# Issuing the eight late stores of each group of results from ACT's queue and no longer from SP's

## The chip, the cores and the metric

The kernel runs on one core of one Trainium2 chip. The metric is the device time of one execution in microseconds (us). The version before takes 1500.18 us (the median of three runs, 1498.26 to 1500.47).

Engines are called as in the profile: PE multiplies matrices, DVE does elementwise work on vectors, ACT applies a function or a scale while it copies, POOL does a few elementwise additions, and SP does no arithmetic; until now it is the queue from which nearly all transfers are issued. A transfer (DMA) is started by an instruction in some engine's queue. The instruction waits there, in order with the rest of that queue, until what it needs is ready; then it hands the transfer to the DMA engines and the queue goes on. The transfer lands some time later.

## The reference

```python
x: (8, 2048, 2048) float32      w: (2048, 2048) float32
cs   = cumsum(x, axis=1)
diff = cs - (cs shifted by one row)
out  = matmul(diff, w)          # (8, 2048, 2048) float32
```

The difference of a running sum is the input itself, so what has to be computed is x times w: 16384 rows of x, each of 2048 numbers, times a matrix of 2048 by 2048.

## The kernel before

The 16384 rows are 128 tiles of 128 rows. The first tiles go through code of their own (a plain product while w is loaded, then two transitional groups). From tile 12 on the work is done in 29 **groups** of four tiles, called g, h, k and l. One group is a product of two-by-two blocks that is computed by seven block products (`P1` to `P7`, the Strassen-Winograd scheme) in place of eight. Most of them are split again by the same scheme into seven quarter products (`P7.p1` to `P7.p7` and so on), so that PE has less to multiply and DVE, ACT and POOL have more to add.

For each tile of a group the following steps run:

- `load` fetches a tile of x in two halves into slots of the buffer `F` (line 113, SP).
- `weigh0` and `weigh1` run over the two halves on ACT and give sums of absolute values (line 125). From them comes a scale for each row (`scale`, `recip`, `unit`, on POOL and DVE).
- `narrow0` and `narrow1` scale the tile and round it to 16 bits, in place in `F` (line 172, ACT).
- `turn0` and `turn1` are transfers that transpose the rounded tile from `F` into one of the tiles `x00` to `x31` (line 185, SP). A slot of `F` can be loaded again when the transposes that read it have landed.

The results of a group are 16 pieces of 128 by 512 numbers: `C11`, `C12`, `C21` and `C22`, each with `g0`, `g1`, `h0` and `h1`. A piece is collected in one of seven buffers `c0` to `c6`. ACT copies the first partial product into the buffer (`keep`), DVE adds others (`add`), and at last the piece is stored (`put`, line 614). The list of free buffers is a queue: `put` hands its buffer back, and the next step that needs one takes the oldest, so that the next writer of a buffer has to wait until the store that reads it has landed. The same seven buffers also serve as scratch for the copies that ACT makes of partial products (`P7.c1`, `P7.c5`, `P7.c6`, `P7.c7`, line 1086).

Eight of the 16 pieces are scaled **late** (the list `LATE`): they are collected without their row scale, by plain copies (`keep`, line 1116) and plain additions (`add`, line 1127), and ACT multiplies the finished piece by the row scale in place (`last`, line 600). The other eight are scaled at each step, and the last to touch them is DVE.

The order of all this is written out by hand in the table `ORDER`. It names each step of a group and how many groups ahead of the others it runs; the program goes through the table once per group. The helper `after` chains the instructions of each engine in that order, so every engine's queue is in the order of the table. The last group has no late pieces and an order of its own (`END_ORDER`).

Of the kernel before, what the change touches and what calls it, by code (L numbers as in the profile page):

```python
# [10 lines left out]
def kernel(  # L11
# [6 lines left out]
    nc = tc.nc  # L18
    P = 128
# [7 lines left out]
    NB = 512  # L27
# [19 lines left out]
    out2 = out.rearrange("b s d -> (b s) d")  # L47
# [38 lines left out]
    def after(engine, ask):  # L86
        if engine in last:
            with tc.issue_after(last[engine].ins):
                said = ask()
        else:  # L90
            said = ask()
        last[engine] = said[-1] if isinstance(said, tuple) else said
        return said
# [100 lines left out]
    with ExitStack() as head:  # L194
# [103 lines left out]
        def put(c, rows, columns, queue=nc.gpsimd):  # L298
            return queue.dma_start(out2[rows, columns], c)
# [86 lines left out]
        with tc.issue_after(whole_max.ins):  # L386
            for c, rows, columns in done:
                put(c, rows, columns)
# [21 lines left out]
        def left_over(ps):  # L410
            for ko in range(KO):
                after(
                    "pe",
                    lambda: nc.tensor.matmul(
                        ps,
                        xP[:, PLAIN - 1, ko, :],
                        (B11, B21)[ko // KH][ko % KH][:, 1, :],
                        start=(ko == 0),
                        stop=(ko == KO - 1),
                    ),  # L420
                )
            c = turned_x[3][0].rearrange("p k m -> p (k m)").bitcast(f32)
            after("act", lambda: nc.scalar.activation(c, ps, COPY, scale=uw))
            rows = ds((PLAIN - 1) * P, P)
            after("sp", lambda: put(c, rows, ds(NB, NB), nc.sync))
# [37 lines left out]
        for c, rows, columns in (done[0], done[3]):  # L463
            after("sp", lambda: put(c, rows, columns, nc.sync))
# [134 lines left out]
    def keep(c, p, u):  # L599
        after("act", lambda: nc.scalar.activation(c, p, COPY, scale=u))  # L600
# [9 lines left out]
        for n in range(2):  # L610
            add(c[n], p[n], u)

    def put(c, t, at):
        after("sp", lambda: nc.sync.dma_start(out2[ds(t * P, P), ds(at * NB, NB)], c))  # L614
        free.append(c)

    store = put
# [370 lines left out]
    class Group:  # L988
# [145 lines left out]
        def put(self, c):  # L1134
            n = 2 * (c[2] == "2") + int(c[4])
            if c in self.late:
                self.step(f"last.{c}", lambda: keep(self.at[c], self.at[c], unit[self.row(c)]))
            self.step(f"put.{c}", lambda: put(self.at.pop(c), self.row(c), n))

        def plan(self):  # L1140
            tiles = self.tiles
# [226 lines left out]
```

## Time and profile before

| what | value |
|---|---|
| median of three runs | 1500.18 us (1498.26 to 1500.47) |
| the profiled execution | 1502.03 us, of which the span from the first to the last instruction is 1500.3 us |
| granted PE clock, mean over the span | 0.997 |
| busy share of the span | PE 96%, DVE 94%, ACT 77%, POOL 35% |
| DMA issues on SP | 246 loads of x, 246 transposes, 492 stores out of `c` buffers, and those of the first tiles |
| DMA | 351.65 MB, mean 234 GB/s; the queue fed by SP was in work for 85.0% of the time of 16 DMA engines |

The groups are alike: between 245 us and 1450 us there are 27 passes through the table, 44.6 us each. So what one pass shows can be multiplied by 27, if the groups of rows show the same wait that many times.

In the rows, a line number is that of the kernel before; "idle before" or a bracket behind an instruction is the time its engine stood still before it, with what ended that wait. "SPq" is SP's queue of DMA issues; "ACTq" is the sequencer of ACT, which handles waits and issues ahead of the arithmetic. `W` is the space of the weights, `flow`, `inner` and `S` are scratch.

### The profile page before, as it was taken

To read this page: it belongs to the slowest core of one execution; us is meant where nothing else is said; L and a number is where in the kernel's file an instruction comes from. 1 tells how busy PE (TensorE), PEld (TensorE's weight loads), DVE (VectorE), ACT (ScalarE), POOL (GpSimd) and SP (SyncE) were. 2 spreads that over 40 slices of the span, in tenths; PEclk is the share of its full clock that TensorE was granted. 3 is DMA by queue.
4 is the path that set the end of the run, shared out by engine and by line. 5 is a ranking of instruction groups with operands and counts; after the bars stand their busy time and mean duration, and the time that the engine had idled before them with its cause. 6 is when DMAs were issued, how large, how long until landed. Compare 5 with 4: busy or idle time off the path is not lost.

```text
span 1500.3 us, 21260 instructions
## 1 busy us (share of the span) xinstructions
PE 1442.9 (96%) x6563; PEld 634.9 (42%) x6563; DVE 1405.8 (94%) x2280; ACT 1154.3 (77%) x1786; POOL 520.0 (35%) x509
## 2 busy tenths in 40 slices
PE   8999989999999999999999999999999999999997
PEld 3444434444444444444444444444444444444443
DVE  7998899999999999999999999999999999999998
ACT  5887467778778788778788778788778777788883
POOL 0111234334434334434334334334334334343342
PEclk9999999999999999999999999999999999999999
DMA  9999758988988988888988888888888988889883
GB/s 363 359 240 282 200 156 223 239 230 219 249 229 219 254 230 224 242 234 222 245 219 227 242 230 229 249 212 241 237 227 238 248 207 232 231 226 247 232 217 126
DMA packets 377761, 351.65 MB, mean 234 GB/s; under 512 B 274800, under 2 KB 274800, under 8 KB 377520
## 3 DMA queue, kind: packets, MB, share of 16 engines
q1 hardware_dynamic: 377088, 348.47, 85.0%
q0 software_dynamic: 560, 1.84, 0.3%
q8 instruction: 51, 0.84, 0.2%
q14 instruction: 62, 0.51, 0.1%
HBM read 150.99 MB, written 134.22 MB: 190 GB/s over the span
## 4 chain that ended last, share of the span: by engine, by line
PE 41%; DVE 28%; DMA 16%; issue 6%; ACT 6%; SPq 2%; POOL 0%; ACTq 0%; DVEq 0%
PE b L592 28%; PE b L573 10%; DVE flow L958 8%; DMA F<-in_x_dram 7%; DVE b L1061 6%; DMA out_dram<-c 6%; DVE c L1127 6%; DVE c L603 4%; PE b L289 3%; DMA x<-F 2%; ACT c L600 2%; DVE x L563 2%; DVE inner L563 1%; SPq L614 1%; ACT waste L125 1%
## 5 line engine op out<-in xcount | busy, mean ns | idle before, releaser
L592 PE MATMUL b<-W,x 128*128 128x512 f16 x2124 | 508.3, 379 | 28.1 <-DVE c L1127 17.0
L592 PEld LDWEIGHTS <-x 128*128 128x128 f16 x2952 | 286.8, 98 | 389.6 <-issue 43.0
L1127 DVE TENSOR_TENSOR c<-b,c 128x512 f32<-128x512 f32 x504 | 325.1, 679 | 2.1 <-ACT c L1116 1.6
L125 ACT ACTIVATE waste<-F 128x1024 uint8<-128x1024 f32 x246 | 259.6, 1055 | 78.7 <-DMA F<-in_x_dram 77.2
L592 PEld LDWEIGHTS <-inner 128*128 128x128 f16 x1996 | 191.7, 98 | 268.0 <-DVE inner L563 25.2
L592 PE MATMUL b<-W,inner 128*128 128x512 f16 x1176 | 289.0, 380 | 9.1 <-DVE b L1061 4.8
L172 ACT ACTIVATE F<-F,of 128x1024 f16<-128x1024 f32 x246 | 282.8, 1150 | 15.9 <-DVE of L156 12.8
L573 PE MATMUL b<-W,x 128*128 128x512 f16 x1216 | 278.0, 379 | 4.1 <-DVE x L563 4.1
L603 DVE SCALAR_TENSOR_TENSOR c<-b,of,c 128x512 f32<-128x512 f32 x286 | 207.8, 742 | 30.4 <-ACT c L600 24.2
L600 ACT ACTIVATE c<-b,of 128x512 f32<-128x512 f32 x268 | 180.2, 679 | 72.1 <-issue 26.6
L561 POOL TENSOR_TENSOR x<-x,x 128x512 f16<-128x512 f16 x87 | 128.9, 1482 | 274.1 <-DVE inner L563 258.4
L1116 ACT COPY c<-b 128x512 f32<-128x512 f32 x224 | 127.6, 582 | 116.2 <-DVE c L603 41.2
L563 DVE TENSOR_TENSOR x<-x,x 128x1024 f16<-128x1024 f16 (+1 forms) x330 | 200.3, 613 | 16.5 <-DMA x<-F 13.4
L592 PE MATMUL b<-flow,x 128*128 128x512 f16 x820 | 210.3, 379 | 0.2
L958 DVE TENSOR_TENSOR flow<-W 128x2048 f16<-128x2048 f16 x145 | 201.9, 1392 | 0.1
L1061 DVE TENSOR_TENSOR b<-b,c 128x512 f32<-128x512 f32 x290 | 192.3, 691 | 4.8 <-ACT c L1086 3.4
L561 POOL TENSOR_TENSOR inner<-inner,x 128x512 f16<-128x512 f16 x58 | 89.0, 1535 | 292.6 <-DVE inner L563 287.2
L573 PEld LDWEIGHTS <-x 128*128 128x128 f16 x1216 | 118.3, 98 | 149.5 <-DVE x L563 9.4
L561 POOL TENSOR_TENSOR inner<-x,inner 128x512 f16<-128x512 f16 x87 | 125.6, 1443 | 121.2 <-DVE inner L563 69.8
L600 ACT ACTIVATE c<-c,of 128x512 f32<-128x512 f32 x224 | 155.9, 718 | 1.1 <-DVE c L1127 1.1
L142 POOL TENSOR_SCALAR of<-of 128x1 f32<-128x1 f32 x112 | 96.4, 861 | 123.6 <-ACT waste L125 123.6
L592 PE MATMUL b<-inner 128*128 128x512 f16 x472 | 116.4, 379 | 0.0
(78 smaller groups left out, 959.2 us busy)
## 6 DMA issues: line engine op xcount, KB each, us to landing
F<-in_x_dram SPq DMA_DIRECT2D x246, 512.0 KB, 5.8
out_dram<-c SPq DMA_DIRECT2D x492, 256.0 KB, 3.2
W<-in_w_dram SPq DMA_DIRECT2D x32, 512.0 KB, 9.7
W<-in_x_dram SPq DMA_DIRECT2D x16, 256.0 KB, 7.2
x<-F SPq DMA_TRANSPOSE x246, 3.3
out_dram<-o POOLq DMA_DIRECT2D x5, 256.0 KB, 4.1
out_dram<-o SPq DMA_DIRECT2D x5, 256.0 KB, 3.5
xP<-in_x_dram SPq DMA_DIRECT2D x1, 1024.0 KB, 5.7
```

The source lines that it names most:

```text
L125: lambda: nc.scalar.activation(waste, where[t][i], ABS, scale=1.0 / ROW, accum_out=sums_of[t][:, i : i + 1],),
L172: lambda: nc.scalar.activation(narrowed(t)[:, ds(i * NH, NH)], where[t][i], COPY, scale=s),
L561: after("pool", lambda: nc.gpsimd.tensor_tensor(dst.all, p.all, q.all, op))
L563: after("dve", lambda: nc.vector.tensor_tensor(dst.all, p.all, q.all, op))
L573: said = nc.tensor.matmul(to[n], a[k], b[k][:, n, :], start=(first and k == 0), stop=(k == KH - 1), skip_group_check=True,)
L592: said = nc.tensor.matmul(to, a[k], b[k], start=(first and k == 0), stop=(k == 3), skip_group_check=True)
L600: after("act", lambda: nc.scalar.activation(c, p, COPY, scale=u))
L603: after("dve", lambda: nc.vector.scalar_tensor_tensor(c, p, u, c, MUL, ADD))
L958: after("dve", lambda: nc.vector.tensor_tensor(in_twos(flow), x, y, op))
L1061: after("dve", lambda: nc.vector.tensor_tensor(t, p, s, ADD))
L1116: after("act", lambda: nc.scalar.copy(to, p))
L1127: after("dve", lambda: nc.vector.tensor_tensor(to, p, to, ADD))
```

## The change

`put` gets an argument for the queue. The eight late pieces are stored from ACT's queue, chained behind the ACT instruction that precedes their `put` in the table; the other eight stay on SP. Nothing else is edited: the table, the buffers, the sizes and the arithmetic are as before. There are 28 groups with late pieces, so 224 of the 492 stores move. The last group, which has none, is as it was.

```diff
-    def put(c, t, at):
-        after("sp", lambda: nc.sync.dma_start(out2[ds(t * P, P), ds(at * NB, NB)], c))
+    def put(c, t, at, by="sp"):
+        queue = dict(sp=nc.sync, act=nc.scalar)[by]
+        after(by, lambda: queue.dma_start(out2[ds(t * P, P), ds(at * NB, NB)], c))
         free.append(c)
...
             if c in self.late:
                 self.step(f"last.{c}", lambda: keep(self.at[c], self.at[c], unit[self.row(c)]))
-            self.step(f"put.{c}", lambda: put(self.at.pop(c), self.row(c), n))
+            by = "act" if c in self.late else "sp"
+            self.step(f"put.{c}", lambda: put(self.at.pop(c), self.row(c), n, by))
```

Two places of the instruction order matter for what follows; both are in the pass whose rows are shown later (778 us to 823 us of the trace). The first is SP's queue where the second half of a group's results leaves and the tiles g and h of a later group are loaded. Here `F<-in_x_dram` is a load (two per tile), `out_0_dram<-c3_759` the store of buffer `c3`, and `x31_70<-F_62` a transpose. Before:

```order
L185 DMA_TRANSPOSE x30_69<-F_62 128x8x128
L185 DMA_TRANSPOSE x31_70<-F_62 128x8x128
L614 DMA out_0_dram<-c3_759 128x512
L614 DMA out_0_dram<-c0_747 128x512
L113 DMA F_62<-in_x_dram 128x1024 x2
L614 DMA out_0_dram<-c4_763 128x512
L614 DMA out_0_dram<-c5_767 128x512
L614 DMA out_0_dram<-c6_771 128x512
L113 DMA F_62<-in_x_dram 128x1024 x2
L614 DMA out_0_dram<-c1_751 128x512
L185 DMA_TRANSPOSE x00_63<-F_62 128x8x128
```

And now:

```order
L185 DMA_TRANSPOSE x30_69<-F_62 128x8x128
L185 DMA_TRANSPOSE x31_70<-F_62 128x8x128
L113 DMA F_62<-in_x_dram 128x1024 x4
L615 DMA out_0_dram<-c1_751 128x512
L185 DMA_TRANSPOSE x00_63<-F_62 128x8x128
```

The five stores of `c3`, `c0`, `c4`, `c5` and `c6` (the pieces C11h1, C21h1, C12g1, C21g1 and C11g1) have left SP's queue, and the four half loads of tiles g and h stand directly behind the transposes.

The second place is ACT's queue over the same stretch. `c0_747<-b0_784` is a copy of PSUM bank 0 into `c0`; `waste` is the output of `weigh` that nobody reads; the line numbers of the new kernel are one higher than before from line 615 on. Before:

```order
L600 ACTIVATE c6_771<-c6_771,of_6129 128x512
L600 ACTIVATE c5_767<-c5_767,of_5978 128x512
L125 ACTIVATE waste_61,of_6502<-F_62 128x1024
L1116 COPY c0_747<-b0_784 128x512
L125 ACTIVATE waste_61,of_6502<-F_62 128x1024
L1086 COPY c4_763<-b1_785 128x512
L1116 COPY c5_767<-b5_789 128x512
L1086 COPY c6_771<-b4_788 128x512
L1086 COPY c4_763<-b1_785 128x512
L172 ACTIVATE F_62<-F_62,of_6502 128x1024
L125 ACTIVATE waste_61,of_6574<-F_62 128x1024
L600 ACTIVATE c6_771<-b7_791,of_6351 128x512
```

And now:

```order
L600 ACTIVATE c6_771<-c6_771,of_6129 128x512
L600 ACTIVATE c5_767<-c5_767,of_5978 128x512
L125 ACTIVATE waste_61,of_6502<-F_62 128x1024
L615 DMA out_0_dram<-c5_767 128x512
L1117 COPY c0_747<-b0_784 128x512
L125 ACTIVATE waste_61,of_6502<-F_62 128x1024
L1087 COPY c4_763<-b1_785 128x512
L615 DMA out_0_dram<-c6_771 128x512
L1117 COPY c5_767<-b5_789 128x512
L1087 COPY c6_771<-b4_788 128x512
L1087 COPY c4_763<-b1_785 128x512
L172 ACTIVATE F_62<-F_62,of_6502 128x1024
```

The store of `c6` now stands two instructions ahead of the copy that overwrites `c6` (`P7.c5`), in the same queue, and behind the copy `P7.c1` into `c4`; the store of `c5` stands behind `weigh0` of tile g.

## The prediction

> **What bounds the kernel now.** I read the stretches first (does one engine fill the time?), then the waits of the repeating part, then the instructions of one pass through the table, engine by engine, and last the chain of work. The table by stretches, for the 27 equal passes from 245 to 1450 us; the columns behind the length are busy us of PE, PE's weight loads, DVE, ACT and POOL:
>
> ```profile
> core 0: us, PE busy (x) PEld busy (x) DVE busy (x) ACT busy (x) POOL busy (x), PEclk, DMA share, GB/s
> 245.00:1450.00 1205.00, 1168.43 (x5310) 513.12 (x5309) 1143.58 (x1886) 960.58 (x1515) 463.55 (x454) 1.00 0.87 232
> ```
>
> PE is busy for 1168.4 of 1205 us. Its idle time there is 36.6 us, 1.35 us a pass, so nothing that this change does to the repeating part can gain more than 36.6 us. The question is which of PE's short stops hang on a store or a load. The waits of the same stretch (us in total, times, longest), and below them one of SP's own queue:
>
> ```profile
> ACT waste L125 <- DMA F<-in_x_dram: 72.5, 62, 3.1
> ...
> ACT c L1116 <- DMA out_dram<-c: 23.8, 20, 3.3
> DVE c L603 <- ACT c L600: 22.9, 25, 2.4
> ...
> ACT c L1086 <- DMA out_dram<-c: 10.4, 31, 0.6
> ```
>
> ```profile
> SPq L614 <- ACT c L600: 79.6, 78, 4.0
> ```
>
> ACT waits for loads, and for stores that must land before their buffer is overwritten; DVE waits for an ACT copy once in nearly every pass (25 times). SP stands 79.6 us in front of stores whose scaling on ACT isn't done. One pass shows how these hang together. SP's queue:
>
> ```profile
> 778.14 2.62 SPq L185 DMA_TRANSPOSE x<-F  x2
> 781.39 0.81 SPq L614 DMA_DIRECT2D out_dram<-c  x2
> 782.30 0.90 SPq L113 DMA_DIRECT2D F<-in_x_dram  x2
> 783.24 3.70 SPq L614 DMA_DIRECT2D out_dram<-c  x3
> 786.98 1.51 SPq L113 DMA_DIRECT2D F<-in_x_dram  x2
> ```
>
> The five stores at 781.39 and 783.24 are C11h1, C21h1, C12g1, C21g1 and C11g1, all late. After C12g1 the queue stands until 786.1, when ACT has scaled C21g1, and only then come C11g1 and the loads of tile h. ACT over the same time:
>
> ```profile
> 784.76 1.33 ACT L600 ACTIVATE c<-c,of 128x512 f32<-128x512 f32 x2
> 787.70 1.06 ACT L125 ACTIVATE waste<-F 128x1024 uint8<-128x1024 f32 x1 [1.61 <-DMA F<-in_x_dram]
> ...
> 789.23 1.06 ACT L125 ACTIVATE waste<-F 128x1024 uint8<-128x1024 f32 x1
> ...
> 790.73 0.59 ACT L1086 COPY c<-b 128x512 f32<-128x512 f32 x1 [0.36 <-DMA out_dram<-c]
> 791.22 0.59 ACT L1116 COPY c<-b 128x512 f32<-128x512 f32 x1
> 791.91 1.10 ACT L1086 COPY c<-b 128x512 f32<-128x512 f32 x2
> ...
> 795.70 1.06 ACT L125 ACTIVATE waste<-F 128x1024 uint8<-128x1024 f32 x1 [1.64 <-DMA F<-in_x_dram]
> ...
> 796.75 0.67 ACT L600 ACTIVATE c<-b,of 128x512 f32<-128x512 f32 x1
> ```
>
> Two waits for loads, 1.61 us for tile g and 1.64 us for tile h, and a copy (790.73, `P7.c1`) that waits for C12g1 to land. The copy at 796.75 (`keep.C22g1`) is the one that DVE and through it PE wait for:
>
> ```profile
> 797.46 0.75 DVE L603 SCALAR_TENSOR_TENSOR c<-b,of,c 128x512 f32<-128x512 f32 x1 [1.10 <-ACT c L600]
> ```
>
> ```profile
> 788.57 1.89 PE L592 MATMUL b<-W,x 128*128 128x512 f16 x8
> ...
> 797.95 1.02 PE L592 MATMUL b<-W,x 128*128 128x512 f16 x4 [0.38 <-ACT c L1086]
> ...
> 808.57 5.34 PE L592 MATMUL b<-W,x 128*128 128x512 f16 x24 [0.57 <-DVE c L1127]
> ```
>
> So in each pass one late load of tile h makes ACT late, ACT makes DVE late by 1.10 us, and PE loses 0.38 and 0.57 us behind them. That is where the change is worth something or nothing.
>
> **What the change removes.** SP loses five stores in this place and with them the stand until 786.1. The loads of tile g can go when the transposes are issued, at 780.8 (778.14 + 2.62), 1.5 us before 782.30. Those of tile h need the slots of `F` that the same two transposes read:
>
> ```profile
> x<-F SPq DMA_TRANSPOSE x246, 3.3
> ```
>
> A transpose lands 3.3 us after its issue; the second is issued at about 779.5, so tile h's loads go at about 782.8, 4.2 us before 786.98. Even if the time from the first issue to the last landing stays 8.7 us (786.98 to 795.70), the second half lands at about 791.5, before ACT asks for it at 794.1 (795.70 less 1.64). Both waits for loads go, in this sum.
>
> **What is late next: ACT's own store.** C11g1 is now issued from ACT behind `P7.c1`, and two instructions later `P7.c5` overwrites its buffer. I call X the start of `P7.c1`, L the time from issue to landing, D the start of `P7.c5`: D = X + L + 0.1 (the semaphore, about what the trace leaves between landing and start). Before, X is 790.73 and D is 791.91; the end of `keep.C22g1` (796.75 + 0.67 = 797.42) is 5.51 us after D, of which 1.64 us is the wait for the load. Without that wait it is D + 3.87. DVE is ready at 796.36 (797.46 less 1.10). So DVE's wait is gone for D up to 792.5, and is what it was at D = 793.55: **the change gains while X + L is below 793.45, and loses above.**
>
> X: `P7.c1` needs PE's first four of the eight products at 788.57 (789.6 with the semaphore), C12g1's landing, and `weigh1` of tile g in front of it on ACT. With tile g's loads 1.5 us earlier `weigh0` is bound by the end of the two scalings (784.76 + 1.33 = 786.1), and `weigh1` ends by 789.2. So X lies between 789.6 and the 790.73 of now. I take 789.6, PE's bound, since the loads move by more than the 1.1 us between them.
>
> L is not shown for a store from ACT. The rows nearest to it, all stores of the repeating part and then C21g1 and C11g1 alone (issue ns, then us to landing, each as min, median, max):
>
> ```profile
> L614 SPq DMA_DIRECT2D out_dram<-c x424: 332/408/1805, 250.9 to 1448.0; - x142
> DMA to landing us min/median/max: 2.3/3.3/8.8
> ```
>
> ```profile
> L614 SPq DMA_DIRECT2D out_dram<-c x2: 343/388/432, 786.1 to 786.5; - x2
> DMA to landing us min/median/max: 5.0/5.2/5.3
> ```
>
> The bounds are 2.3 and 5.3. I take the median, 3.3: by 789.6 the loads that these two stood behind have had their 1.5 to 4.2 us of lead. Then D = 789.6 + 3.3 + 0.1 = 793.0, `keep.C22g1` ends at 796.87, and DVE waits 0.5 us in place of 1.1. **0.55 us a pass, in the 25 passes that have the wait: 14 us.** PE can follow: its two stops are 0.95 us together. At L = 2.3 the whole 22.9 us of the row goes.
>
> The page "DMA: Bandwidth & Descriptors" of the Trainium skill (section "Queues, rings and completion order") says that SP and ACT each have a ring of their own on the same 16 DMA engines, and that an engine goes round the rings packet by packet. By that rule a store from ACT is not behind SP's loads, and the sum holds or comes out better; in the trace all these transfers were in one ring, so it doesn't show it.
>
> **The issue on ACT.** 224 stores at a median of 0.41 us are 91 us that move from SP to ACT. I cost them at nothing, because each stands behind at least one ACT instruction that isn't the scaling it waits for, and ACT's sequencer runs ahead of its arithmetic. In the chain of work ACTq handles the waits of two later instructions while the `weigh1` of 795.70 still runs and `keep.C22g1` hasn't begun:
>
> ```profile
> 796.07 0.02 ACTq L1086
> ...
> 796.38 0.02 ACTq L125
> ```
>
> The shortest cover is a copy of 0.59 us over 0.41 us. Without the cover, two issues (C21g1 and C11g1) lie on the way to D: 0.82 us a pass. Three of the eight stores also inherit a wait for a semaphore that a transpose on SP used eight transfers earlier; a transpose lands 3.3 us after issue, so that is long past, and costs something only if SP falls behind ACT.
>
> The other late stores: C11h1 and C21h1 go when they do now; C12g1 goes just ahead of the scalings at 784.76, some 1.5 us after its 783.24 of now, but the 7 us that it takes to land now (until just before 790.73) are spent behind tile g's loads. Copies into the buffers of the other five wait for a landing 20 times now, 23.8 us in all, 0.9 us a pass. That can go or, if these stores land later, as much can come; ACT has 9 us idle in a pass (1205 less 960.6 over 27) to take it up. I put it at nothing.
>
> **The rivals.**
>
> *ACT waits for its own store (slower).* If the transfers don't land sooner, because the DMA engines are the limit (0.87 busy in the row of stretches), X stays 790.73. With L = 3.3, D = 794.1: 0.6 us too late, 27 times, 16 us, 1516 us. With L = 5.3, D = 796.1 and 2.6 us a pass: 70 us, 1570 us. For it: the copies at 790.73 and 791.91 start when a store has landed even now. Against it: that landing is of a store that sat behind the loads in one queue.
>
> *The issue isn't hidden on ACT (slower).* 0.82 us less the 0.55 gained is 0.27 a pass, 7 us: 1507 us. If an issue from ACT must wait for one from SP, it is more; a transpose holds SP for 1.3 us (2.62 for two), so at worst twice that on the way: 2.1 us a pass, 56 us, 1556 us. The page "Perfetto Trace Analysis" of the Trainium skill (section "DMA Instruction — HWDGE") speaks for this: the generator of descriptors is one for both queues, and is locked while one uses it. No run here shows it yet; in the pass above SP is done with its transposes at 780.8, before the first late store.
>
> *Nothing (same).* The loads and stores share the DMA engines in another order, and the last of them lands when it did. Then ACT's waits only change their names: 1500 us, give or take 3. The Trainium skill's page "DMA: Bandwidth & Descriptors" (section "Issuing engines are not separate DMA queues") says against this change that issuing from several engines saves no more than the issuing time, as all use the same 16 DMA engines. SP's issuing time bounds nothing here, so by this rule alone there is no gain. What speaks against it is the stand of SP until 786.1, which is order and not bandwidth.
>
> **How the numbers follow.** The profiled execution took 1502.03 us, 0.1% above the median of 1500.18; the sum is made against the median. Forecast: 1500.2 - 14 = **1486 us**. Its own range runs from 22.9 us and a few more of PE's 36.6 us gained (1474) to a gain at the limit of what can be told (1497); a measurement of this kernel can tell about 0.2%, 3 us. Chances: the forecast 0.48, ACT's own store 0.27, the issue not hidden 0.12, nothing 0.13. Faster comes from the forecast alone, less the part of it under 3 us, and a little of "nothing": 0.47. Same: 0.12. Slower: 0.41. The range from 1474 to 1524 takes in the first third of the slower cases, and leaves out their worse ends.
>
> **What would show it.** Right: SP issues four half loads in one run behind the transposes; ACT's wait for loads falls from 72.5 us to under 20; `DVE c L603 <- ACT c L600` falls to about 13; ACT L1086 waits for `out_dram<-c` for 2.3 us a pass (793.0 less X and two copies), about 60 us in place of 10.4; PE's idle time in the repeating part about 23 us. Wrong: that wait of L1086 at 3 us a pass or more with L603 waiting longer than 22.9 us (the first rival); ACT instructions starting late behind a store with no semaphore named (the second); loads that land no earlier (the third).

## The result, and the profile after

The changed kernel takes **1549.56 us** (median; 1548.95 to 1550.83), the kernel before 1499.30 us beside it: a ratio of 1.0336, 95% interval 1.0318 to 1.0354. It is slower by 50 us, where 14 us less were forecast, and lies above the range. From line 615 on, a line of the kernel has a number one higher than before (L614 is L615, L1086 is L1087, L1116 is L1117, L1127 is L1128).

The stretch of the equal passes is now 1252 us long. By the starts of the same copy (`keep.C22g0`) 25 passes apart, a pass takes 47.2 us (1178.9 over 25) in place of 45.4 (1134.1 over 25); the 44.6 us stated ahead of the prediction came from counting 27 passes in a stretch that holds 26.6. The table by stretches of the changed kernel, columns as before:

```profile
245.00:1497.00 1252.00, 1175.13 (x5314) 512.76 (x5312) 1133.95 (x1891) 956.90 (x1519) 473.11 (x454) 1.00 0.81 223
```

PE is idle for 76.9 us of it (1252 less 1175.1), against 36.6 before; the DMA engines' share has fallen from 0.87 to 0.81, so over the stretch as a whole they have more time to spare than before. The waits of the same stretch (us in total, times, longest):

```profile
ACT c L1117 <- DMA out_dram<-c: 156.3, 81, 5.5
...
DVE c L1128 <- ACT c L1117: 39.6, 53, 1.8
PE b L592 <- ACT c L1087: 32.7, 44, 2.2
ACT c L1087 <- DMA out_dram<-c: 29.9, 44, 2.0
...
DVE c L603 <- ACT c L600: 9.5, 24, 0.4
...
ACT waste L125 <- DMA F<-in_x_dram: 4.3, 3, 2.5
```

The last two rows are what was meant to shrink, and did: ACT's wait for loads fell from 72.5 to 4.3 us, DVE's wait for ACT from 22.9 to 9.5. The first row is new in size: before a `keep` copy overwrites a buffer, ACT waits 156.3 us for a store of results to land, where it was 23.8. DVE waits for those copies, PE for the copies of L1087 behind them.

One pass, SP's queue first, and then ACT:

```profile
799.67 2.62 SPq L185 DMA_TRANSPOSE x<-F  x2
802.40 2.91 SPq L113 DMA_DIRECT2D F<-in_x_dram  x4
811.07 0.34 SPq L615 DMA_DIRECT2D out_dram<-c  x1
```

```profile
802.21 0.72 ACT L600 ACTIVATE c<-c,of 128x512 f32<-128x512 f32 x1 [0.16 <-DVE c L1128]
802.84 0.67 ACT L600 ACTIVATE c<-b,of 128x512 f32<-128x512 f32 x1
802.96 0.37 ACTq L615 DMA_DIRECT2D out_dram<-c  x1
804.34 0.69 ACT L600 ACTIVATE c<-b,of 128x512 f32<-128x512 f32 x1 [0.84 <-PE b L592]
804.37 0.34 ACTq L615 DMA_DIRECT2D out_dram<-c  x1
809.08 0.59 ACT L1117 COPY c<-b 128x512 f32<-128x512 f32 x1 [4.04 <-DMA out_dram<-c]
809.09 0.34 ACTq L615 DMA_DIRECT2D out_dram<-c  x1
...
814.83 0.59 ACT L1117 COPY c<-b 128x512 f32<-128x512 f32 x1 [0.79 <-DMA out_dram<-c]
815.83 1.07 ACT L1087 COPY c<-b 128x512 f32<-128x512 f32 x2 [0.41 <-DMA out_dram<-c]
```

SP issues the four half loads in one run, as forecast. The stores at 802.96 and 804.37 are C11h1 and C21h1. The copy at 809.08 is `keep.C12g0`: it overwrites the buffer of C11h1, and ACT stands 4.04 us until that store has landed. The row of that one store (issue ns, then us to landing), and the row of the same store in the pass shown of the kernel before:

```profile
L615 ACTq DMA_DIRECT2D out_dram<-c x1: 366/366/366, 803.0 to 803.0; - x1
...
DMA to landing us min/median/max: 6.0/6.0/6.0
```

```profile
L614 SPq DMA_DIRECT2D out_dram<-c x1: 338/338/338, 781.4 to 781.4; - x1
...
DMA to landing us min/median/max: 2.5/2.5/2.5
```

Following each store and load through 24 whole passes of the two traces gives this (medians, us from issue to landing; "by" is the time from the issue of the named load's last half to that of the store; the last three columns say which copy overwrites the buffer, and what ACT waits there for that store, us in all):

| store | before | after | what is ahead of it after | copy that waits | before | after |
|---|---|---|---|---|---|---|
| C11h1 | 2.57 | 5.60 | first half of load.g, by 0.2 us | keep.C12g0 | 17.3 | 86.5 |
| C21h1 | 4.17 | 6.96 | load.g, by 0.8 us | keep.C12g1 | 0 | 3.9 |
| C12g1 | 7.13 | 4.83 | load.g and load.h, by 3.6 us | P7.c1 | 4.5 | 12.4 |
| C21g1 | 5.05 | 4.44 | load.h, by 5.5 us | keep.C12h1 | 3.0 | 19.4 |
| C11g1 | 5.57 | 2.35 | no load | P7.c5 | 4.6 | 14.9 |
| C12g0 | 4.09 | 5.79 | load.k, by 0.5 us | keep.C21g1 | 0 | 23.2 |
| C12h0 | 2.99 | 2.57 | no load | P1.ct | 1.0 | 0 |
| C12h1 | 4.19 | 5.11 | load.l, by 1.7 us | keep.C11h1 | 0 | 7.1 |

On SP, C11h1, C21h1, C12g0 and C12h1 stood ahead of the loads. From ACT they are issued when ACT comes to them, and SP, which stands for none of them any more, has issued its loads by then.

The changed kernel even holds both cases of C11h1. In 22 of 27 passes the first half of load.g was issued before it, mostly by 0.21 us, and it landed in 5.3 to 7.2 us, mostly 0.18 us behind that load. In the other 5 the store went first, by 0.03 to 0.67 us, and it landed in 3.6 to 4.5 us.

### The profile page after: what moved, and what is told of

It is laid out like the page before. It is cut to its first block, busy times and chain, and to the rows that moved or that the text cites. A ratio compares the mean times of both kernels' runs of the same rounds, so it can differ in the third digit from the quotient of the medians.

```text
span 1547.0 us, 21258 instructions
## 1 busy us (share of the span) xinstructions
PE 1449.6 (94%) x6563; PEld 634.0 (41%) x6563; DVE 1394.0 (90%) x2280; ACT 1148.6 (74%) x1786; POOL 528.2 (34%) x509
## 4 chain that ended last, share of the span: by engine, by line
DMA 38%; PE 22%; ACT 19%; DVE 14%; issue 6%; POOL 1%; ACTq 0%; SPq 0%; DVEq 0%; POOLq 0%
DMA out_dram<-c 34%; PE b L592 13%; PE b L573 6%; ACT F L172 6%; ACT c L600 5%; DVE b L1062 4%; ACT waste L125 3%; DVE c L603 3%; DVE flow L959 3%; PE b L289 3%; ACT c L1117 2%; DMA x<-F 2%; DVE c L1128 2%; ACT c L1087 1%; ACT b L1055 1%
## 5 line engine op out<-in xcount | busy, mean ns | idle before, releaser
L592 PE MATMUL b<-W,x 128*128 128x512 f16 x2124 | 513.1, 380 | 13.7 <-ACT b L1055 4.8
L1128 DVE TENSOR_TENSOR c<-b,c 128x512 f32<-128x512 f32 x504 | 327.9, 682 | 42.3 <-ACT c L1117 41.3
L1117 ACT COPY c<-b 128x512 f32<-128x512 f32 x224 | 128.2, 586 | 226.1 <-DMA out_dram<-c 162.2
L573 PE MATMUL b<-W,x 128*128 128x512 f16 x1216 | 279.7, 381 | 9.8 <-DVE x L563 9.8
L561 POOL TENSOR_TENSOR x<-x,x 128x512 f16<-128x512 f16 x87 | 154.3, 1774 | 285.5 <-DVE inner L563 241.8
L600 ACT ACTIVATE c<-b,of 128x512 f32<-128x512 f32 x268 | 181.0, 681 | 71.8 <-PE b L592 29.7
L603 DVE SCALAR_TENSOR_TENSOR c<-b,of,c 128x512 f32<-128x512 f32 x286 | 207.8, 742 | 18.3 <-ACT c L600 10.9
L1062 DVE TENSOR_TENSOR b<-b,c 128x512 f32<-128x512 f32 x290 | 192.2, 690 | 22.9 <-ACT c L1087 16.1
L573 PEld LDWEIGHTS <-x 128*128 128x128 f16 x1216 | 118.8, 98 | 156.3 <-DVE x L563 16.6
L959 DVE TENSOR_TENSOR flow<-W 128x2048 f16<-128x2048 f16 x145 | 177.5, 1224 | 0.1
L600 ACT ACTIVATE c<-c,of 128x512 f32<-128x512 f32 x224 | 155.9, 718 | 1.4 <-DVE c L1128 1.1
L142 POOL TENSOR_SCALAR of<-of 128x1 f32<-128x1 f32 x112 | 73.0, 652 | 179.7 <-ACT waste L125 179.7
## 6 DMA issues: line engine op xcount, KB each, us to landing
W<-in_w_dram SPq DMA_DIRECT2D x32, 512.0 KB, 10.1
```

The source lines that it names most:

```text
L561: after("pool", lambda: nc.gpsimd.tensor_tensor(dst.all, p.all, q.all, op))
L573: said = nc.tensor.matmul(to[n], a[k], b[k][:, n, :], start=(first and k == 0), stop=(k == KH - 1), skip_group_check=True,)
L592: said = nc.tensor.matmul(to, a[k], b[k], start=(first and k == 0), stop=(k == 3), skip_group_check=True)
L603: after("dve", lambda: nc.vector.scalar_tensor_tensor(c, p, u, c, MUL, ADD))
L959: after("dve", lambda: nc.vector.tensor_tensor(in_twos(flow), x, y, op))
L1062: after("dve", lambda: nc.vector.tensor_tensor(t, p, s, ADD))
```

## The experiments

Two theories. **ORDER**: a transfer lands behind what was issued shortly ahead of it, whichever queue it came from; the change turned the order of stores and loads round. **QUEUE**: a store from ACT's queue is slow in itself beside SP's loads. Medians of landings and sums of waits by step are over the same 24 passes as in the table. The kernel before ran at 1499.5 to 1502.7 us beside each of these. In e3, e4, e9, e10, e13, e14 and e15 the mean granted PE clock was lower too (0.948 to 0.984, and 0.993 or more in the others), and over the same 25 passes PE was busy for 1119 to 1147 us with the products that took it 1087 to 1110 us in the others. So up to some 45 us of those seven times are not waits; why the clock was lower no run shows.

### e1_two_back: C11h1 and C21h1 back on SP

```diff
-            by = "act" if c in self.late else "sp"
+            by = "act" if c in self.late and c in ON_ACT else "sp"   # ON_ACT: the other six
```

> C11h1 and C21h1 go back to SP's queue, where they stand ahead of the loads of tile g; the other six late stores stay on ACT's queue. Two theories. ORDER: a transfer lands behind what was issued ahead of it, whichever queue it came from; in the changed kernel load.g was issued 0.2 us ahead of C11h1, so C11h1 landed in 5.6 us instead of 2.6, and keep.C12g0 waited 3.6 us a pass for it. Then here C11h1 lands in 2.5 to 3 us again, ACT's wait at that copy falls under 1 us a pass, the sum of `ACT c <- DMA out_dram<-c` over the keep copies from 162 us to under 80, and the time lies between 1485 and 1515 us. QUEUE: a store from ACT's queue is slow in itself beside SP's loads. Then the six left on it keep their 4 to 6 us, the waits stay above 120 us in all, and the time stays between 1530 and 1560 us.

Measured: 1554.34 us, ratio 1.0375 (1.0350 to 1.0400). C11h1 lands in 2.55 us and `keep.C12g0` waits as it did before, as ORDER had it; but its time is missed by 40 us, and the keep copies wait 95.6 us in all where it had under 80. The waits of this kernel (copies of L1088 and L1118, one line further down):

```profile
ACT c L1118 <- DMA out_dram<-c: 95.6, 63, 4.0
PE b L592 <- ACT c L1088: 64.9, 51, 2.7
ACT c L1088 <- DMA out_dram<-c: 59.4, 46, 3.1
```

The wait has moved: `P7.c1` stands 44.9 us for C12g1, which is now issued 0.4 us behind the last of four half loads and lands in 7.56 us; `keep.C12h1` 29.0 us for C21g1 (6.20 us); `keep.C21g1` 29.1 us for C12g0. The two stores from ACT with no load ahead, C11g1 and C12h0, land in 2.61 and 2.54 us. That speaks against QUEUE, whose time was right.

### e2_same_order: the changed kernel's order, from one queue

```diff
-    ... put.C11h1+1 keep.C22g0+1 put.C21h1+0 ... load.g+2 ...
+    ... keep.C22g0+1 ... load.g+2 put.C11h1+1 load1.g+2 put.C21h1+0 ...   # load.g: first half, load1.g: second
```

> All stores on SP, but issued there in the order in which the changed kernel issued them from two queues: first half of load.g, C11h1, second half of load.g, C21h1. ORDER: C11h1 lands in 5.3 to 6 us, just as it did from ACT's queue (5.6); keep.C12g0 waits 3 to 4 us a pass; SP still stands for the scaling of C21g1, so the loads of tile h are late as well and the time is 1545 to 1600 us. QUEUE: SP's queue isn't slow, C11h1 lands in under 4 us, and the time is that of before, 1495 to 1515 us. If instead a queue of its own shields a store from the loads' packets, C11h1 lands later here than in the changed kernel, at 6.5 us or more.

Measured: 1519.18 us, ratio 1.0141 (1.0119 to 1.0162). C11h1 lands in 4.98 us from SP, behind the load in all 27 passes, and `keep.C12g0` waits 86.6 us for it, as in the changed kernel (86.5). So no queue of ACT is needed for that wait. The time is 26 us below the range: the loads of h still stand on SP behind C21g1 and C11g1, which land in 2.64 and 3.31 us (5.05 and 5.57 before), and `weigh0.g` waits no more. C11h1 lands no later here than from ACT: a queue of its own did not make it land sooner.

### e3_hold and e4_load_early: load.g later, and sooner

```diff
-    ... put.C21h0+0 ... put.C11g0+1 turn0.l+1 turn1.l+1 ...
+    ... turn0.l+1 turn1.l+1 put.C21h0+0 put.C11g0+1 ...     # e3
```

```diff
-    ... turn0.l+1 turn1.l+1 ... load.g+2 ...
+    ... load.g+2 turn0.l+1 turn1.l+1 ...                    # e4
```

> The changed kernel, with the stores of C21h0 and C11g0 (both on SP) moved behind the second transposition of tile l: they take the places that C11h1 and C21h1 had on SP, so that load.g is issued about 0.9 us later, as in the kernel before, and 0.9 us behind C11h1 and not 0.2 us ahead of it. ORDER: C11h1 lands in 2.6 to 4.4 us (that is what the five passes of the changed kernel show in which it was issued first), keep.C12g0 waits under 2 us a pass, the time falls by 20 to 50 us, to 1500 to 1530. QUEUE: C11h1 takes 5 us or more as before, and the time stays within 1540 to 1560 us.

> The changed kernel, with load.g moved on SP ahead of the transpositions of tile l, some 5 us earlier, so that it has nearly landed when C11h1 is issued from ACT. ORDER: C11h1 lands in 2.5 to 4 us, keep.C12g0 waits under 1.5 us a pass; against that the transpositions of tile l land 2 to 3 us later, behind 1 MB of loads; 1485 to 1530 us. QUEUE: C11h1 takes 5 us beside load.h; 1540 us or more.

Measured: 1660.44 us (1.1083, 1.1047 to 1.1120) and 1675.32 us (1.1178, 1.1151 to 1.1205). Neither made the case it was to make. In e3 `keep.C11h0` overwrites the buffer of C21h0, which is now stored later:

```profile
ACT c L600 <- DMA out_dram<-c: 119.5, 53, 5.6
```

ACT stands there 84 us in all, so that C11h1 is issued 2.2 us behind load.g and not ahead of it; it lands in 7.15 us. In e4 the transpositions of tile l stand behind 1 MB of loads, and DVE and PE wait for the tile:

```profile
DVE x L563 <- DMA x<-F: 166.6, 31, 8.3
...
PE b L573 <- DVE x L563: 145.3, 27, 7.6
```

In e4 C11h1 lands in 6.59 us, where ORDER had 2.5 to 4, and `keep.C12g0` still waits 116 us for it. By then load.g has 2.7 us to go, but the second transposition of tile l, issued 1.6 us ahead of the store, takes 9.0 us to land behind load.g (3.1 in the changed kernel). That it is what holds the store is argued from these numbers, not tested. Neither run tells ORDER from QUEUE.

### e5_two_only: only C11h1 and C21h1 from ACT

ON_ACT holds these two.

> Only C11h1 and C21h1 are issued from ACT; the other six late stores are on SP as before. The order of issue about load.g is then close to that of e2_same_order (load.g at the same moment as C11h1, C21h1 behind it, the loads of tile h behind the scaling of C21g1), but from two queues. ORDER (a transfer lands behind those issued ahead of it, whatever the queue): C11h1 lands in 5 to 5.8 us, keep.C12g0 waits 3 to 4 us a pass, and the time is within 10 us of e2_same_order's 1519. QUEUE (a store from ACT's queue is slow in itself): C11h1 lands in over 6 us, and the time is over 1535 us.

Measured: 1533.30 us (1527.10 to 1535.34), ratio 1.0201 (1.0171 to 1.0232). C11h1 lands in 5.56 us and `keep.C12g0` waits 86.7 us, as in e2. The two kernels differ in the queue alone, or nearly, and have the same wait; in 4 passes C11h1 is issued first and lands in 3.4 to 4.9 us. The time is 14 us above e2's and not within 10, and below the 1535 of QUEUE. Over the same 25 passes PE is idle for 56.0 us, 48.3 in e2; the row in which it waits for sums of transposed tiles (L573) is 5.9 us larger, as in e18 below.

### e6_mid_three: only C12g0, C12h0, C12h1 from ACT

ON_ACT holds these three.

> Only C12g0, C12h0 and C12h1 are issued from ACT, the three that the prediction put at nothing because ACT is idle for 9 us a pass. C12g0 is then issued 0.2 us behind load.k and no longer 0.5 us ahead of it, and lands in 5.8 us and not 4.1. If a wait of ACT costs its full length (the copy keep.C21g1 waits 29 us in all for that store in e1_two_back), the time is 1515 to 1530 us. If ACT's idle time takes it up, as the prediction had it, the time is 1497 to 1503 us, or a little less for the earlier loads.

Measured: 1513.11 us, ratio 1.0074 (1.0046 to 1.0102), 2 us below the first range and far from the second. C12g0 lands in 5.80 us, and `keep.C21g1` waits 27.5 us for it. Before, the same copy waited 15.8 us for PE; its whole wait grows from 15.8 to 29.5 us, by 13.7. `keep.C11h1` waits 10.1 us where it didn't wait before, 8.3 of them for C12h1. ACT's idle time in all grows by 12.4 us (221.2 to 233.6 over the same passes), and the kernel by 11 to 13. So about half of these 23.8 us was taken up where other waits of ACT shrank, and the other half reached the time.

### e7_store_early: the late stores sooner on ACT

```diff
-    ... narrow0.l+1 ... put.C11h1+1 ... put.C21h1+0 ... put.C12g1+0 ...
+    ... narrow0.l+1 put.C21h1+0 ... put.C11h1+1 put.C12g1+0 ...
```

> The changed kernel, all eight on ACT, but C21h1 is issued right behind narrow0.l, some 5 us sooner (it has been scaled by then), and C12g1 right behind C11h1, 5 us sooner. keep.C12g0 then overwrites the buffer of C21h1, which has long landed. ORDER: the wait of 3.6 us a pass at keep.C12g0 goes, and most of that of P7.c1; left are those at keep.C12h1, P7.c5 and keep.C21g1, 20 to 30 us each; 1490 to 1520 us. QUEUE: the wait only moves to the next copies, 1535 us or more.

Measured: 1534.70 us, ratio 1.0211 (1.0182 to 1.0241): 15 us below the changed kernel's median, but above the range. `keep.C12g0` waits for no store any more (it waited 86.5 us). C12g1 holds `P7.c1` for no more than 2.4 us. But `keep.C12h1` waits 51.2 us, in place of 19.4, for C21g1, which ACT now issues 3.4 us behind the last half of load.h (5.5 us in the changed kernel) and which lands in 5.78 us. The time is at the edge of what QUEUE forecast; the wait is again at a store that a load was issued ahead of.

### e8_sp_fix, e11_sp_swap, e12_sp_c21: the order on SP put right

```diff
-                self.step(f"load.{c}", lambda t=t: (load(t, 0), load(t, 1)))
+                self.step(f"load.{c}", lambda t=t, o=c == "h": (load(t, o), load(t, 1 - o)))   # e8, e11
```

```diff
-    ... put.C11g0+1 ... put.C11h1+1 keep.C22g0+1 put.C21h1+0 ...
+    ... put.C11g0+1 put.C21h1+0 ... put.C11h1+1 keep.C22g0+1 ...                               # e8, e12
```

> The kernel before, all stores on SP, with two changes of order there: C21h1 is issued right behind C11g0, 5 us sooner, so that one store less stands ahead of load.g; and of tile h's two half loads the second goes first, since ACT weighs the second half first. ORDER: load.g goes 0.4 us sooner and has the engines to itself sooner, the wait of weigh0.g falls from 1.4 us a pass to under 1, that of weigh1.h (1.1 us) goes, the part of keep.C12g0's wait that is for a store (17 us in all) goes: 1470 to 1490 us. If ACT's waits for loads are not what PE waits for, the time stays within 1496 to 1503 us.

> The kernel before with one edit: of tile h's two half loads the second is issued first, since ACT weighs the second half first. It takes away the wait of weigh1.h alone (26 us in 25 passes), which the prediction put at the head of the chain to DVE's 22.9 us. If that chain is right, DVE's wait for keep.C22g1 falls under 10 us and the time by 12 to 23 us, to 1477 to 1488. If the late load of h isn't what PE waits for, the time stays within 3 us of before.

> The kernel before with the other edit of e8_sp_fix alone: C21h1 is issued on SP right behind C11g0, 5 us sooner, and so isn't ahead of load.g any more. If the order of issue is what counts, weigh0.g's wait for load.g falls from 1.4 to about 1 us a pass, as in e8, and keep.C12g0 waits for no store (17 us in all before): the time falls by 10 to 25 us, to 1475 to 1490, the rest of e8's 36 us. If it is nothing, 1497 to 1503.

Measured: e8 1463.91 us (0.9748, 0.9727 to 0.9769), e11 **1462.66 us** (0.9757, 0.9736 to 0.9778), e12 1494.69 us (0.9965, 0.9951 to 0.9978). Loading tile h's second half first, all stores on SP, is worth 38 us alone, and e11 and e8 are the fastest kernels here; sending C21h1 sooner is worth 6 us alone, less than the 10 to 25 expected, and nothing on top of it. e8 is 6 us and e11 14 us below the forecast range. The table by stretches and the waits of e11:

```profile
245.00:1415.00 1170.00, 1158.12 (x5330) 517.72 (x5328) 1126.44 (x1895) 963.18 (x1521) 482.35 (x455) 1.00 0.89 240
```

```profile
DVE c L603 <- ACT c L600: 1.0, 4, 0.4
```

PE's idle time is 11.9 us in place of 36.6, and DVE's wait of 22.9 us is 1.0. The chain from the late load of h through ACT and DVE to PE, on which the prediction stood, is shown; only there was a cheaper way to break it.

### e9_hold_h and e10_act_all: a wrong edit

> e7_store_early (all eight on ACT) with one step moved: the loads of tile h stand on SP behind the store of C11h0, which waits for DVE, so that they are issued behind C21g1 and no longer 5 us ahead of it. ORDER (a transfer lands behind those issued ahead of it, whatever the queue): C21g1 lands in 2.5 to 4 us and not 5.8, the 51 us that keep.C12h1 waits in e7 fall under 15, and the time comes back to 1495 to 1515 us, although all eight stores are still on ACT's queue. QUEUE (ACT's queue is slow in itself): C21g1 stays over 5 us, the time over 1525 us.

> e9_hold_h with the two other stores that landed late issued sooner: C12g0 right behind keep.C22g1 (ahead of load.k), C12h1 right behind weigh1.k (ahead of load.l); and of tile h's half loads the second first, since ACT weighs it first. ORDER: the 30 us that keep.C21g1 waits for C12g0 go, and so does the wait of weigh1.h; 1465 to 1490 us, below both kernels and near e8_sp_fix's 1464. QUEUE: over 1500 us.

Measured: 1598.37 us (1.0656, 1.0628 to 1.0685) and 1610.67 us (1.0740, 1.0711 to 1.0769). I had moved load.h behind `weigh1.h` in the table. That weighing then reads the half that stood there before, and SP stands until it is done (SP's waits in e9):

```profile
SPq L113 <- ACT waste L125: 228.0, 26, 9.8
```

These two times say nothing on the theories. One landing does: in e10 C12g0, from ACT with no load ahead, takes 2.41 us.

### e13_hold_h2, e14_act_all2, e15_sp_h_first: the order changed on both queues

```diff
-    ... P7.c5+0 ... load.h+1 ... put.C11h0+0 ...
+    ... P7.c5+0 ... put.C11h0+0 load.h+1 ...          # e13, on top of e7; e14: C12g0, C12h1 sooner, h's halves swapped
```

```diff
-    ... load.h+1 ... load.g+2 P6h.3+1 keep.C12g0+1 S3.g+1 put.C12g1+0 ...
+    ... load.g+2 load.h+2 P6h.3+1 keep.C12g0+1 S3.g+1 put.C12g1+0 ...   # e15, all stores on SP
```

> What e9_hold_h was to show: e7_store_early (all eight on ACT, C21h1 and C12g1 issued sooner), with the store of C11h0 moved on SP ahead of the loads of tile h. SP then waits there for DVE until about the moment at which ACT issues C21g1, so that C21g1 goes ahead of these loads and no longer behind them. ORDER (a transfer lands behind those issued ahead of it, whatever the queue): C21g1 lands in 2.5 to 4 us and not 5.8, the 51 us that keep.C12h1 waits for it in e7 fall under 15, the time comes back to 1495 to 1515 us with all eight stores on ACT. QUEUE (ACT's queue is slow in itself): C21g1 stays over 5 us, the time over 1525.

> e13_hold_h2 with C12g0 issued right behind keep.C22g1 (ahead of load.k), C12h1 right behind weigh1.k (ahead of load.l), and tile h's second half loaded first. ORDER: the 30 us that keep.C21g1 waits for C12g0 go, and the wait of weigh1.h; 1465 to 1490 us with all eight stores on ACT. QUEUE: over 1500 us.

> All stores on SP, with the loads of tile h moved there ahead of C12g1, C21g1 and C11g1: the order of issue of e1_two_back (1554 us), from one queue. ORDER: C12g1 lands in 7 to 8.5 us, P7.c1 and keep.C12h1 wait over 1 us a pass each for a store, and the time is 1530 to 1560 us without one store on ACT's queue. QUEUE: the loads of h come early and the stores don't suffer on SP; 1480 to 1505 us.

Measured: e15 1559.17 us, ratio 1.0371 (1.0322 to 1.0421). With not one store on ACT, it is as slow as e1 (1554) and the changed kernel (1550). C12g1 lands in 8.59 us behind the loads of h, and `P7.c1`, a copy of L1086, waits 65 us for it, 45 in e1. `keep.C12h1`, which was to wait over 1 us a pass, waits 0.7 us in all. That the times of e1 and e15 agree is in part chance: over the same 25 passes PE is idle for 78.8 us in e1 and 70.9 in e15, and busy for 1105 and 1119 us, at a mean granted clock of 0.994 and 0.977.

```profile
ACT c L1086 <- DMA out_dram<-c: 73.2, 29, 3.7
DVE b L1061 <- ACT c L1086: 68.6, 27, 3.8
PE b L592 <- ACT c L1086: 65.4, 27, 3.7
```

e13 is at 1657.63 us (1.1046, 1.1007 to 1.1085), e14 at 1605.47 us (1.0700, 1.0673 to 1.0728), both far above the range. In e13 the store that I had meant does what ORDER says: C21g1 lands in 3.94 us, and `keep.C12h1` waits 14.7 us for it. But the loads of h now stand between C21g1 and C11g1, which lands in 6.85 us where it took 4.0 in e7, and `P7.c5` overwrites its buffer:

```profile
ACT c L1087 <- DMA out_dram<-c: 129.0, 28, 5.9
```

In e14 it is the same store (5.77 us, 94.8 us of waiting at `P7.c5`); C12g0, sooner, lands in 2.88 us, but its buffer is then the next that is free, `keep.C12h0` takes it at once and waits 56.7 us.

### e16_all_ahead, e17_all_ahead_six, e18_six_swap

```diff
-    ... put.C11g1+0 ... last.C21g1+0 ...
+    ... last.C21g1+0 put.C11g1+1 ...      # e16, on top of e13; e17: C12g0 and C12h1 on SP; e18: and h's halves swapped
```

> e13_hold_h2 with C11g1 issued behind last.C21g1, 3 us sooner: in e13 it was the one store that still went behind the loads of tile h, landed in 6.85 us, and P7.c5 waited 117 us for it. All eight are still on ACT. ORDER: C11g1 lands in under 4.5 us, the wait of P7.c5 falls under 25 us, and the time falls by 90 to 150 us, to 1505 to 1565 (the waits for C12g0 and C12h1, behind load.k and load.l, are left). QUEUE: the store stays at over 6 us, and the time over 1630.

> e16_all_ahead with C12g0 and C12h1 back on SP, where they stand ahead of load.k and load.l; six on ACT, all of them issued ahead of the loads of tile h. ORDER: the 30 us that keep.C21g1 waits for C12g0 go as well; 20 to 40 us less than e16. QUEUE: these two gain no more than 10 us, the six left still cost what they did.

> e17_all_ahead_six with tile h's second half loaded first, the edit that took the kernel before from 1500 to 1463 us in e11. In e17 weigh1.h waits 29 us for that half again, since its load was put behind the stores, and DVE waits 36.5 us for the copy behind it: the chain of before. ORDER: both go, and the time falls by 30 to 50 us, to 1485 to 1505; what is then left above e11's 1463 is C21g1 and C12g1, behind load.g. QUEUE: ACT's waits for its own stores bound the kernel; less than 15 us.

Measured: 1543.49 us (1.0288, 1.0264 to 1.0312), 1534.36 us (1.0220, 1.0198 to 1.0242) and 1480.51 us (0.9874, 0.9828 to 0.9920). In e16 C11g1 lands in 4.46 us, `P7.c5` waits 28.7 us for a store and not 117 (under 25 was expected), and 114 us of time are gone, as ORDER said, by moving one issue of a store ahead of a load on the other queue. The row of e13, in e16:

```profile
ACT c L1087 <- DMA out_dram<-c: 36.1, 20, 3.3
```

Two things go with it. The move also exchanges two buffers: `P7.c5` now overwrites that of C21g1, which lands in 5.5 us, and `keep.C12h1` that of C11g1. And not all of the 114 us are waits. The same 25 passes of e13 and of e16, columns as in the tables by stretches:

```profile
290.98:1567.95 1276.97, 1147.16 (x4999) 495.56 (x4998) 1068.15 (x1775) 903.73 (x1425) 444.46 (x425) 0.95 0.77 206
284.64:1459.69 1175.05, 1109.96 (x4997) 483.28 (x4995) 1075.23 (x1775) 901.65 (x1426) 427.53 (x425) 0.99 0.84 224
```

PE's idle time falls by 64.7 us (129.8 to 65.1), its busy time by 37.2 at the higher clock.

e17 gained 9 us and not 20 to 40, which is what QUEUE had forecast (no more than 10): `keep.C21g1` waits for no store any more, but ACT still waits 28.9 us at `weigh1.h` for the load of h, which has stood behind the stores since e13. e18 takes that wait away and gains 54 us, more than the 30 to 50 forecast. With six of the eight stores on ACT's queue it is 22 us faster than the kernel before, which speaks against QUEUE, and 18 us slower than e11, which has the same swap and all stores on SP. Its table by stretches:

```profile
245.00:1430.00 1185.00, 1162.37 (x5324) 517.41 (x5323) 1123.80 (x1893) 961.76 (x1519) 485.86 (x455) 1.00 0.90 236
```

PE is idle for 22.6 us there, 11.9 in e11. In e18 C12g1 and C11h1 are still issued beside load.g, and land in 7.02 and 5.62 us, but the copies that overwrite their buffers wait no more than 0.2 us for them. Most of the difference in idle time stands in one row (e11 first, then e18), where PE waits for sums of transposed tiles:

```profile
PE b L573 <- DVE x L563: 4.4, 6, 1.1
PE b L573 <- DVE x L563: 13.4, 7, 4.4
```

DVE in turn waits for the transposes there, 4.4, 5.1 and 3.2 us in three single passes (0.7, 0.9 and 1.1 at the same places in e11); why they land late in these passes no run shows. Over the same 25 passes PE is also busy for 5 us more (1092.2 and 1087.2). ACT's one larger wait for a late store, 11.0 us at `P7.c5` for C21g1 (0.8 in e11), is not named in these rows. Whether a store from ACT costs anything beyond its place in the order stays open within these 18 us.

Taken together, the landings went as ORDER forecast, or within 0.4 us of it, in e1, e2, e5, e13, e15 and e16, and not in e4. In e3 the case to be tested did not come about. The times went so in e15 and e16 alone; QUEUE's forecast of the time held in e1, e13, e14 and e17, where waiting that was taken away at one step came back at others.

## Why the prediction was wrong

**The step that failed** is "The other late stores", where C11h1 and C21h1 "go when they do now" and what the remaining stores may lose is put at nothing. C11h1 does, within 0.1 us (1.6 us behind the issue of the second transpose of tile l, before and after). C21h1 is issued 0.75 us later (1.98 and 2.73 us behind that transpose), because on ACT it stands behind `keep.C22g0`, which waits for PE. C12g1, which was to go 1.5 us later, goes 3.9 us later, because on ACT it stands behind `keep.C12g0`, which waits for C11h1. And the loads went sooner: the step took the five stores off SP and counted the 1.5 to 4.2 us that the loads gain, without asking which stores the loads then overtake. On SP the table's order had put C11h1 and C21h1 ahead of load.g, C12g0 ahead of load.k and C12h1 ahead of load.l, and each of these buffers is the next to be overwritten. e2 and e15 show that such an order alone, on one queue, makes the waits at `keep.C12g0` and `P7.c1`.

**"ACT has 9 us idle in a pass to take it up"** failed for the most part. Those 9 us are themselves waits between copies that follow each other in a fixed order. Over the 24 passes, ACT's waits for late stores grew by 137 us (30.4 to 167.4, the table's columns), those for loads fell by 55 (`weigh0.g` and `weigh1.h`), and some 32 us fell in with waits that stood there anyway (`keep.C12g0` for PE, `keep.C21h1` for DVE): about 50 us are left, close to the result. In e6, with three stores, about half of the new waits reached the time.

**The first rival** had the right mechanism, ACT waiting for its own store, and the wrong store. It looked at C11g1 alone. That one lands in 2.35 us, at the lower bound of 2.3 to 5.3 and better than the 3.3 taken, since no load is near it. That the rival's two prices, 1516 and 1570 us, have the measured time between them is luck. The row of L1086, forecast at about 60 us, is 29.9 (L1087).

**Right** were these. SP issues four half loads in one run. ACT's wait for loads fell below 20 us (4.3). `DVE c L603 <- ACT c L600` fell below the 13 forecast (9.5). The issue itself costs ACT no time that shows:

```profile
L615 ACTq DMA_DIRECT2D out_dram<-c x224: 337/338/847, 184.8 to 1512.5; - x112
```

It takes 0.34 us (0.41 on SP before) and overlaps the instruction ahead of it, as at 802.96 and 809.09 above. Where a load's issue on SP overlaps one on ACT it takes 0.52 us and not 0.43 (medians of 48 and 174 issues), far less than the second rival's 2.1 us a pass. So that rival was wrong, and the third too: the loads did land sooner.

**The gain** of ending the wait for load.h was mis-sized. The sum had 14 us, with the row of 22.9 as its upper end; e11, which ends that wait and leaves the stores where they were, gains 38. In the stretch PE's idle time fell by 24.7 us (36.6 to 11.9), somewhat more than the row of 22.9, and its busy time by 10.3 (1168.4 to 1158.1); the cause of the second part no run shows. (Over the same 25 passes of both traces the two are 21.7 and 13.2 us.)

The rule that I took from the Trainium skill's page "DMA: Bandwidth & Descriptors" (section "Queues, rings and completion order"), that an engine goes round the rings packet by packet, was to let a store from ACT pass SP's loads. The trace agrees with the rule, but not with what I made of it. Between 900.2 and 902.8 us the first half of load.g (issued at 897.97 us) and the store of C11h1 (issued 0.21 us behind it) are both on their way, and packets (the pieces in which the DMA engines move a transfer, here a row of a tile each) of SP's queue (q1) and of ACT's (q10) run in equal number:

```profile
q1 hardware_dynamic: 143, 0.52, 63.7%
q10 hardware_dynamic: 143, 0.26, 26.2%
```

The store shares the engines with the load and doesn't pass it. By the trace's packet records (medians of 24 passes) its first packet runs 1.75 us after its issue and its last 3.1 us later; C11g1, with no load near, starts after 0.84 us and is through 0.8 us later. In e2, on SP's queue behind the same half load, C11h1 starts after 2.9 us and is through 1.7 us later. So the two queues reach nearly the same landing by different ways. The same page's section "Issuing engines are not separate DMA queues" says that transfers from several engines share the same DMA engines and that only issuing time is saved; here the trace agrees: with nearly the same order from two queues (e1) and from one (e15), PE is idle for 78.8 and 70.9 us over 25 passes.

## What to carry to other kernels

A queue's program order is also a schedule of the DMA engines: before a store is moved to another queue, list the loads that it stood ahead of, and check when its buffer is overwritten, because the loads will be issued first. Idle time of an engine that works through a fixed order is not all slack: in e6 half of the new waits became time. Look first at which half of a transfer its consumer needs first: swapping two half loads was worth 38 us here, and moving eight stores to a free queue cost 50.

## What the runs showed of the hardware

I had not expected that 0.2 us decide some 2 us across two queues. In e5, e7, e16, e17 and e18, as in the changed kernel, a store of C11h1 that ACT issued about 0.2 us behind the first half of load.g landed mostly 0.18 us behind that load, in 5.6 to 5.8 us (medians); in the 4 to 7 passes of each in which it went first, by medians of 0.3 to 0.6 us, it landed in 3.4 to 4.2 us. From SP, with 0.9 us of lead (before, e1, e15), it took 2.6 us. Stores from ACT with no load near landed in 2.3 to 2.6 us (C11g1, C12h0; C21h1 in e7), as they do from SP (C21h1 in e8: 2.4).

The order across the two queues is not strict. In e1 C12g1, from ACT, landed ahead of the half load of h that SP had issued 0.41 us before it, in 23 of 25 passes and by 0.68 us (median); in e15, from SP's own queue, it landed 0.68 us behind that half load in all 25. Transfers issued shortly ahead of a store delay its first packet, whichever queue it is in: from ACT it ran 0.84 us after the issue with no load near, 1.75 us behind one half load (C11h1), 3.7 us behind two (C12g0) and 4.4 us behind four (C12g1 in e1). From then on the packets of the two queues run side by side. Whether the delay arises in the making of the descriptors or in the DMA engines no run shows.
